# One decoder layer on one core: the last expert's order, its combines and the second LayerNorm rearranged, and larger weight transfers up to it

## The chip, the cores and the metric

The kernel runs on one core of a Trainium2 chip. The metric is device microseconds of one execution (us), less being better; the median of three runs before the change is 1119.88 us (1118.96 to 1120.91). The engines that matter here are TensorE (PE in the profile, its weight loads PEld), VectorE (DVE), ScalarE (ACT), GpSimd (POOL) and SyncE (SP), which issues nearly all DMAs.

## The reference, cut to what matters

For 256 tokens of width 1024, a mixing sublayer (two kinds of attention, merged and projected) is followed by a LayerNorm, and then by the sublayer in which the change lies:

```python
logits = (xt @ w_router + b_router)
top_val, top_idx = lax.top_k(logits, 4)              # 4 of 32 experts
gates = jax.nn.softmax(top_val, axis=-1)
# for each expert e and the tokens that chose it:
h = xb @ w_gate_up[e] + b_gate_up[e]                 # 1024 -> 2048
gate = jnp.minimum(gate, 7.0); up = jnp.clip(up, -7.0, 7.0)
act = gate * jax.nn.sigmoid(gate * 1.702) * (up + 1.0)
ys = act @ w_down[e] + b_down[e]                     # 1024 -> 1024
out[token] += ys * gate_weight
# and at the end
y = (xf - mu) * lax.rsqrt(var + LN_EPS) * g + b      # LN2 over alpha * h + moe(h)
```

Everything is float32. The weights of one expert are 8 MB of `w_gate_up` and 4 MB of `w_down`, so that 32 experts read 403 MB.

## The kernel before

**Experts.** A loop (`for e in range(NE)`) runs over 32 experts in order. Each one has room for 64 tokens; tokens beyond that go through a loop of their own after expert 20, which is skipped where there are none. An iteration issues on TensorE, in this order: `up_proj(e)` (eight steps c = 0 to 7, each a MB of weights and four logical products, which write two PSUM tiles G), `combine(e - 2)` (adds the output of the expert before the last to the four accumulators `acc[t][k]`, t for the half of the tokens, k for the half of the 1024 columns), `scatter` (two transposes that turn the weighted one-hot matrix into GT), half of a `gather` for the next pair of experts, the transposes of `swiglu(e)`, and `down(e - 1)`. A float32 product is two MATMUL records in the profile. A product with 64 output rows uses half of the array's columns, and two of them run side by side. After `up_proj`, ScalarE (L860) and VectorE (L858) copy the two tiles G to `G_sb`, which the transposes of `swiglu` read.

**Weights.** From expert 4's down weights on, weights lie in five buffers of 4 MB. An expert's `w_gate_up` is two tiles (the first with the steps c = 0 to 3, the second with 4 to 7), its `w_down` one. The list `items` holds them in the order of use: the two tiles of expert e, then the down tile of expert e - 1. `load_next` calls `fetch`, which issues a tile's DMAs on SP's queue, as soon as the tile five places earlier has been used. A tile goes as one DMA (32 KB in a row per partition), as two (16 KB) in the nine tiles from expert 28's first one to expert 29's down tile, and as four (8 KB) in the next three: the first and second up tile of expert 31, and the down tile of expert 30. A product waits for the DMA that brings the part it reads, not for the tile. The very last tile, the down weights of expert 31, is fetched in six pieces by `fetch_last`.

**The end.** After the loop, `down(31)` is written out in pieces: `last_down(k, c0, c1)` computes column half k for steps c0 to c1, into `pt[k]`, a PSUM tile of 128 x 256 whose upper 64 partitions hold the first 256 columns and whose lower ones the other 256. `last_combine(k)` copies it to both partition halves of D2 in four copies of 64 x 256, ScalarE and VectorE in turn, then TensorE adds D2 to the accumulators in two products of 64 rows and 512 columns, and VectorE takes the statistics of LN2 (`stats`: `bn_stats`, and with k = 1 the aggregate and ScalarE's square root). Then LN2 is applied to the four quarters (t, k) of the output. Three go through VectorE in two instructions each, `scaled` (L1074: subtract the mean, multiply by g) and `shifted` (L1078: multiply by the inverse deviation, add b), and the quarter (0, 1) through ScalarE (L1084) and two instructions of GpSimd (L1086). Each quarter is stored by a DMA of 256 KB.

**Order.** The schedule is manual: each engine runs its instructions in the order in which the program writes them, and waits only for the data they need. The framework that inserts the waits lets two engines use one PSUM bank only in turn.

Of the kernel before, what the change touches and what calls it, by code (L numbers as in the profile page):

```python
# [9 lines left out]
F32 = mybir.dt.float32  # L10
# [8 lines left out]
P = 128  # L19
# [16 lines left out]
def layer(tc, x, w_in, b_forget, sink, w_proj_swa, w_proj_fox, w_out, ln1_g, ln1_b, w_router, b_router,  # L36
# [9 lines left out]
    with ExitStack() as ctx:  # L46
# [71 lines left out]
        items += [("D", NE - 1, q) for q in range(2)]  # L118
        where, nxt, used, big = {}, [0], [0], []

        def fetch(kind, e, q, r, n=1, steps=1):

            src, m = (w_gate_up, 2) if kind == "G" else (w_down, 4)
            src = src[e].rearrange("a (p c) n -> p (a c) n", c=8)[:, m * q:m * q + m * n, :]
            dst, k = r.rearrange("p (c n) -> p c n", c=m * n), m * n // steps
            for i in range(0, m * n, k):
                sp.dma_start(dst[:, i:i + k], src[:, i:i + k])

        def fetch_last(r):

# [7 lines left out]
        def big_tile():  # L138

            return big[(nxt[0] - 2) // 2 % 5].tile([P, 2 * 4096], F32, name="ww", tag="ww")  # L140

        def load_next(n=1):
            for _ in range(n):
                i = nxt[0]
                kind, e, q = items[i]
                if i < SMALL:
                    r = extra.tile([P, 4096], F32, name="w") if i == 10 else slot_tile(slot_of[(i - (i > 10)) % 10])
                    where[kind, e, q] = r
                    fetch(kind, slice(e, e + 1), q, r)
                    nxt[0] += 1  # L150
                    continue
                r = big_tile()
                where[kind, e] = r
                for a in range(2):
                    where[kind, e, q + a] = r[:, 4096 * a:4096 * a + 4096]
                if i + 2 < len(items):
                    fetch(kind, slice(e, e + 1), q, r, 2, 4 if i + 8 >= len(items) else 2 if i + 26 >= len(items) else 1)
                else:
                    fetch_last(r)
                nxt[0] += 2  # L160
# [593 lines left out]
        with tc.tile_pool(name="mo", bufs=1) as mo:  # L754
# [85 lines left out]
                act.activation(GT, pt, AF.Copy)  # L840
                return GT

            def up_proj(xT_e, weights):
                G = [gp.tile([P, 512], F32, name="G") for _ in range(2)]
                for c in range(8):
                    if c % 2 == 0:
                        w = weights("G", c // 2).rearrange("p (c n) -> p c n", c=2)
                    for hf in range(2):
                        for k in range(2):
                            n0 = k * 1024 + hf * 512  # L850
                            pe.matmul(G[hf][64 * k:64 * k + 64, :], xT_e[:, c, :], w[:, c % 2, n0:n0 + 512],  # L851
                                      start=c == 0, stop=c == 7)
                G_sb = mo.tile([P, 8, P], F32, name="G_sb")
                for hf in range(2):
                    dst = G_sb.rearrange("q c p -> q p c")[:, 64 * hf:64 * hf + 64]
                    src = G[hf].rearrange("q (p c) -> q p c", c=8)
                    if hf:
                        dve.tensor_copy(dst, src)  # L858
                    else:
                        act.activation(dst, src, AF.Copy)  # L860
                return G_sb
# [34 lines left out]
            def combine(GT, D_sb, first=False):  # L896
                for t in range(2):
                    for k in range(2):
                        r = slice(64 * k, 64 * k + 64)
                        pe.matmul(acc[t][k], GT[r, t * P:(t + 1) * P], D_sb[r, :], start=first, stop=False)  # L900
# [65 lines left out]
            for e in range(NE):  # L966
                g = e // 2
                OHg = weighted(posm[:, :, e:e + 1], gate[:, :, e:e + 1])
                if e % 2 == 0 and e + 2 <= last:
                    OH = onehot(g + 1)  # L970
                G_sb = up_proj(xTs[g][:, :, e % 2, :], lambda kind, q: where[kind, e, q])
                refill(4, 2 if e == OVER else 0)

                if e > 1 and e != OVER + 1:
                    combine(GTs[e - 2], Ds[e - 2], e == 2)
                if e == NORM:
                    affine()
                    b_dn = mo.tile([NE, D], F32, name="rows")
# [6 lines left out]
                if e == REST:  # L985
# [13 lines left out]
                    rows = mo.tile([NE + 1, D], F32, name="rows")  # L999
                    act.dma_start(rows[0:1], ln2_g)  # L1000
                    act.dma_start(rows[NE:], ln2_b)
                GTs[e] = scatter(OHg)
                if 2 * (g + 1) <= last:
                    gather(g + 1, OH, 4 * (e % 2))
                aTs[e] = swiglu(G_sb, bT[:, :, :, e])
# [12 lines left out]
                if e == OVER:  # L1018
# [3 lines left out]
                    with tc.If(n_ov > 0):  # L1022
                        overflow()
                    refill(0)
            y = big_tile()[:, :2 * D].rearrange("p (t n) -> p t n", t=2)

            mv = mo.tile([P, 2, 2], F32, name="mv2")
            rs = mo.tile([P, 2], F32, name="rs2")
            nm = mo.tile([P, 1], F32, name="nm2")
            stt = mo.tile([P, 2, 2, 6], F32, name="stt2")  # L1030
            cs = [slice(512 * k, 512 * k + 512) for k in range(2)]

            def stats(t, k):
                dve.bn_stats(stt[:, t, k], acc[t][k])
                if k == 1:
                    dve.bn_aggr(mv[:, t], stt[:, t])
                    act.activation(rs[:, t:t + 1], mv[:, t, 1:2], AF.Sqrt, bias=eps)


            wv = where["D", last].rearrange("p (c n) -> p c n", c=8)  # L1040
# [9 lines left out]
            def last_combine(k):  # L1050

                D2 = mo.tile([P, 512], F32, name="tb", bufs=2)
                for r in (slice(0, 64), slice(64, P)):
                    act.activation(D2[r, :256], pt[k][:64], AF.Copy)  # L1054
                    dve.tensor_copy(D2[r, 256:], pt[k][64:])  # L1055
                for t in range(2):
                    r = slice(64 * t, 64 * t + 64)
                    pe.matmul(acc[t][k], GTs[last][r, t * P:(t + 1) * P], D2[r], start=False, stop=True)  # L1058
                for t in range(2):
                    stats(t, k)  # L1060

            for c in (0, 2, 4):
                for k in range(2):
# [2 lines left out]
                    combine(GTs[last - 1], Ds[last - 1])  # L1066
            last_down(0, 6, 8)
            last_down(1, 6, 7)
            last_combine(0)
            last_down(1, 7, 8)  # L1070
            last_combine(1)

            def scaled(t, k):
                dve.scalar_tensor_tensor(y[:, t, cs[k]], acc[t][k], mv[:, t, 0:1], gb[:, 0, cs[k]],  # L1074
                                         op0=OP.subtract, op1=OP.mult)

            def shifted(t, k):
                dve.scalar_tensor_tensor(y[:, t, cs[k]], y[:, t, cs[k]], rs[:, t:t + 1], gb[:, 1, cs[k]],  # L1078
                                         op0=OP.mult, op1=OP.add)
                sp.dma_start(out[t * P:(t + 1) * P, cs[k]], y[:, t, cs[k]])  # L1080

            dve.reciprocal(rs[:, 0:1], rs[:, 0:1])
            dve.scalar_tensor_tensor(nm, mv[:, 0, 0:1], -1.0, rs[:, 0:1], op0=OP.mult, op1=OP.mult)
            act.activation(y[:, 0, cs[1]], acc[0][1], AF.Identity, bias=nm, scale=rs[:, 0:1])  # L1084
            for a, op in ((0, OP.mult), (1, OP.add)):
                pool.tensor_tensor(y[:, 0, cs[1]], y[:, 0, cs[1]], gb[:, a, cs[1]], op=op)  # L1086
            scaled(0, 0)
            dve.reciprocal(rs[:, 1:2], rs[:, 1:2])
            shifted(0, 0)
            for k in range(2):  # L1090
                scaled(1, k)
                shifted(1, k)
            act.dma_start(out[0:P, cs[1]], y[:, 0, cs[1]])


_INS = ['x', 'w_in', 'b_forget', 'sink', 'w_proj_swa', 'w_proj_fox', 'w_out', 'ln1_g', 'ln1_b', 'w_router', 'b_router',
# [24 lines left out]
```

## Time and profile before

| | |
|---|---|
| median of the runs | 1119.88 us |
| profiled execution | 1119.41 us |
| its span, first to last instruction | 1117.2 us |
| PE busy | 1054.9 us (94%) |
| DVE / ACT / POOL busy | 378.3 / 211.3 / 4.8 us |
| TensorE's granted clock, mean | 0.985 of full speed |
| DMA, mean over the span | 387 GB/s; 429 to 432 in most slices of the expert loop |
| idle of PE ahead of `up_proj` (L851) | 19.5 us, of it 19.1 us for weights |

All times of the profile are counted from the first instruction; what the execution has beyond its span is 2.2 us. "Granted clock" is 1.00 at 2.4 GHz and 0.50 at 1.2 GHz. A busy PE means that a matmul is under way, not that the array is full. In a timeline a row is a run of like instructions, with the idle time before it and what ended that in brackets.

### The profile page before, as it was taken

What the parts mean: (1) busy time and instruction counts of PE and PEld (TensorE: products, weight loads), DVE (VectorE), ACT (ScalarE), POOL (GpSimd) and SP (SyncE); (2) the same over time, 40 slices, a digit from 0 to 9 for tenths busy, and PEclk for the clock granted to TensorE, in tenths of its full rate; (3) what the DMA queues carried; (4) which work ended last, traced back from release to release, by engine and by line L of the source; (5) the groups of instructions that cost most, each with busy time, mean ns of one, the idle gap of its engine ahead of it and who ended that gap; (6) DMA issues with size and microseconds to landing.
All of it is one profiled execution on the core that took longest, in us unless ns stands there. A gap on an engine that the chain in (4) does not pass through costs nothing. (4 is left out here: it accounts for less than half of the span.)

```text
span 1117.2 us, 13432 instructions
## 1 busy us (share of the span) xinstructions
PE 1054.9 (94%) x5677; PEld 517.1 (46%) x5677; DVE 378.3 (34%) x821; ACT 211.3 (19%) x416; POOL 4.8 (0%) x14
## 2 busy tenths in 40 slices
PE   9999999999999999999999999999998988998895
PEld 8988897533333333333333343333433333333322
DVE  5577476432222224222222222222222222222223
ACT  5466464311111110000000110011000000000011
POOL 0000000000000000000000000000000000000001
PEclk9999999999999998999999999999999999999997
DMA  9754599999999999999999999999999999999993
GB/s 274 227 195 146 140 392 354 377 426 405 429 424 429 432 431 416 430 429 430 430 430 431 429 432 431 431 431 430 429 429 431 430 429 430 426 425 428 423 419 121
DMA packets 46406, 432.48 MB, mean 387 GB/s; under 512 B 5524, under 2 KB 26020, under 8 KB 29448
## 3 DMA queue, kind: packets, MB, share of 16 engines
q1 hardware_dynamic: 46144, 431.18, 93.5%
q8 instruction: 46, 0.75, 0.3%
q10 hardware_dynamic: 200, 0.41, 0.1%
q14 instruction: 16, 0.13, 0.0%
HBM read 430.53 MB, written 1.05 MB: 386 GB/s over the span
## 5 line engine op out<-in xcount | busy, mean ns | idle before, releaser
L851 PE MATMUL G<-ww,xTe 128*64 128x512 f32 x1664 | 368.2, 597 | 19.5 <-DMA ww<-in_w_gate_up_dram 19.1
L851 PEld LDWEIGHTS G<-ww,xTe 128*64 128x64 f32 x1664 | 119.3, 138 | 264.1 <-issue 227.3
L886 PE MATMUL X<-ww,aT 128*64 128x512 f32 x864 | 191.3, 595 | 0.5 <-DVE tb L871 0.3
L858 DVE COPY G_sb<-G 128x512 f32<-128x512 f32 x32 | 33.2, 1037 | 408.0 <-PE G L851 408.0
L860 ACT ACTIVATE G_sb<-G 128x512 f32<-128x512 f32 x32 | 33.8, 1055 | 422.3 <-PE G L851 422.3
L886 PEld LDWEIGHTS X<-ww,aT 128*64 128x64 f32 x864 | 59.6, 137 | 113.4 <-issue 107.6
L851 PE MATMUL G<-w,xTe 128*64 128x512 f32 x384 | 83.5, 593 | 0.6 <-POOL nth L773 0.6
L312 PE MATMUL pj<-w 128*128 128x256 f32 x232 | 66.7, 288 | 1.3 <-ACT w L110 0.8
L314 PE MATMUL pj<-w 128*128 128x256 f32 x232 | 65.7, 283 | 0.2 <-DVE w L111 0.2
L313 PE MATMUL pj<-w 128*128 128x256 f32 x232 | 65.6, 283 | 0.0
L809 PE MATMUL X<-OH,h_perm 128*128 128x128 f32 x480 | 63.0, 288 | 1.2 <-DVE h_perm L947 0.9
L900 PE MATMUL acc<-D_sb,GT 64*128 64x512 f32 x248 | 61.6, 615 | 0.7 <-DVE D_sb L893 0.7
L809 PEld LDWEIGHTS X<-OH,h_perm 128*128 128x128 f32 x480 | 60.1, 204 | 1.8 <-PE X L839 1.2
L868 PE MATMUL X<-ident,G_sb 128*128 128x128 f32 x256 | 40.0, 280 | 20.1 <-ACT xTe L822 12.0
L873 ACT ACTIVATE sg<-tb 128x256 f32<-128x256 f32 x64 | 26.7, 416 | 148.5 <-DVE tb L872 148.5
L851 PEld LDWEIGHTS G<-w,xTe 128*64 128x64 f32 x384 | 28.3, 137 | 53.6 <-issue 52.3
L893 DVE COPY D_sb<-X 128x256 f32<-128x256 f32 x31 | 13.2, 425 | 112.0 <-ACT D_sb L892 112.0
L111 DVE TENSOR_TENSOR w<-w 128x1024 fp32r<-128x1024 f32 (+2 forms) x50 | 46.3, 965 | 13.8 <-ACT w L110 13.8
L312 PEld LDWEIGHTS pj<-w 128*128 128x128 f32 x232 | 44.3, 191 | 3.9 <-issue 2.2
L871 DVE TENSOR_TENSOR tb<-X,bT 128x512 f32<-128x512 f32 x64 | 43.7, 683 | 4.1 <-PE X L868 4.1
L314 PEld LDWEIGHTS pj<-w 128*128 128x128 f32 x232 | 44.4, 191 | 0.4 <-DVE w L111 0.4
L313 PEld LDWEIGHTS pj<-w 128*128 128x128 f32 x232 | 44.4, 191 | 0.0
(263 smaller groups left out, 866.6 us busy)
## 6 DMA issues: line engine op xcount, KB each, us to landing
ww<-in_w_gate_up_dram SPq DMA_DIRECT2D x44, 4096.0 KB, 27.2
ww<-in_w_down_dram SPq DMA_DIRECT2D x23, 4096.0 KB, 28.2
w<-in_w_gate_up_dram SPq DMA_DIRECT2D x24, 2048.0 KB, 10.0
ww<-in_w_gate_up_dram SPq DMA_DIRECT2D x12, 2048.0 KB, 38.5
w<-in_w_down_dram SPq DMA_DIRECT2D x8, 2048.0 KB, 10.7
w<-in_w_in_dram SPq DMA_DIRECT2D x14, 1024.0 KB, 5.6
ww<-in_w_down_dram SPq DMA_DIRECT2D x6, 2048.0 KB, 39.7
ww<-in_w_gate_up_dram SPq DMA_DIRECT2D x8, 1024.0 KB, 28.3
```

The source lines that it names most:

```text
L111: dve.tensor_tensor(lo, src, hi.bitcast(F32), op=OP.subtract)
L312: pe.matmul(pt[:, j, :], hi[:, c, cs], xh[:, c, :], start=c == 0, stop=False)
L313: pe.matmul(pt[:, j, :], hi[:, c, cs], xl[:, c, :], start=False, stop=False)
L314: pe.matmul(pt[:, j, :], lo[:, c, cs], xh[:, c, :], start=False, stop=c == 7)
L809: pe.matmul(pt[:, c, :], h_perm[:, t, c0 + c, :], OH[:, t].rearrange("p a s -> p (a s)"), start=t == 0, stop=t == 1)
L851: pe.matmul(G[hf][64 * k:64 * k + 64, :], xT_e[:, c, :], w[:, c % 2, n0:n0 + 512], start=c == 0, stop=c == 7)
L858: dve.tensor_copy(dst, src)
L860: act.activation(dst, src, AF.Copy)
L868: pe.transpose(pt[:, c].rearrange("p k s -> p (k s)"), G_sb[:, c0 + c, :], ident)
L871: dve.tensor_tensor(tb, pt, bias[:, c0:c0 + 4, :, None].to_broadcast([P, 4, 2, CAP]), op=OP.add)
L886: pe.matmul(pt[64 * k:64 * k + 64, :], aT[:, c, :], w[:, c % 4, k * 512:(k + 1) * 512], start=c == 0, stop=c == 7)
L900: pe.matmul(acc[t][k], GT[r, t * P:(t + 1) * P], D_sb[r, :], start=first, stop=False)
```

## The change

The diff has four parts. (1) Every weight tile up to expert 31's first up tile goes as one DMA; its second up tile goes as DMAs of 1, 1 and 2 MB; expert 30's down tile stays at four. (2) For the last expert alone, `combine(29)` and `scatter(31)` are issued inside `up_proj`, ahead of its step 6, rather than after it. (3) Both pieces of `last_down(1, ...)` come ahead of `last_combine(0)`, and each `last_combine` goes by column halves j: ScalarE and VectorE copy the same 64 x 256 piece of PSUM to D2's two partition halves, and then both tokens' halves t are added, 64 rows by 256 columns each. (4) In LN2, the quarters (0, 0), (0, 1) and (1, 0) are finished on TensorE: a PSUM tile `base` first gets the row b by a product with a row of ones (one row deep), a diagonal matrix of the inverse deviation times the scaled quarter is added to it, and ScalarE copies the sum out; the quarter (1, 1) stays on VectorE, and GpSimd has no part any more.

```diff
-        def fetch(kind, e, q, r, n=1, steps=1):
+        def fetch(kind, e, q, r, n=1, *parts):
...
-            dst, k = r.rearrange("p (c n) -> p c n", c=m * n), m * n // steps
-            for i in range(0, m * n, k):
-                sp.dma_start(dst[:, i:i + k], src[:, i:i + k])
+            dst, i, unit = r.rearrange("p (c n) -> p c n", c=m * n), 0, m * n // max(sum(parts), 1)
+            for k in parts or (1,):
+                sp.dma_start(dst[:, i:i + k * unit], src[:, i:i + k * unit])
+                i += k * unit
...
+                steps = {-6: (1, 1, 2), -4: (1, 1, 1, 1)}
...
-                    fetch(kind, slice(e, e + 1), q, r, 2, 4 if i + 8 >= len(items) else 2 if i + 26 >= len(items) else 1)
+                    fetch(kind, slice(e, e + 1), q, r, 2, *steps.get(i - len(items), (1,)))
...
-            def up_proj(xT_e, weights):
+            def up_proj(xT_e, weights, beside=None):
...
+                    if c == 6 and beside:
+                        beside()
...
+                def others():
+                    if e > 1 and e != OVER + 1:
+                        combine(GTs[e - 2], Ds[e - 2], e == 2)
+                    if e == last:
+                        GTs[e] = scatter(OHg)
+                G_sb = up_proj(..., others if e == last else None)
...
             def last_combine(k):
                 D2 = mo.tile([P, 512], F32, name="tb", bufs=2)
-                for r in (slice(0, 64), slice(64, P)):
-                    act.activation(D2[r, :256], pt[k][:64], AF.Copy)
-                    dve.tensor_copy(D2[r, 256:], pt[k][64:])
-                for t in range(2):
-                    r = slice(64 * t, 64 * t + 64)
-                    pe.matmul(acc[t][k], GTs[last][r, t * P:(t + 1) * P], D2[r], start=False, stop=True)
-                for t in range(2):
-                    stats(t, k)
+                for j in range(2):
+                    src, c = pt[k][64 * j:64 * j + 64], slice(256 * j, 256 * j + 256)
+                    act.activation(D2[:64, c], src, AF.Copy)
+                    dve.tensor_copy(D2[64:, c], src)
+                    for t in range(2):
+                        r = slice(64 * t, 64 * t + 64)
+                        pe.matmul(acc[t][k][:, c], GTs[last][r, t * P:(t + 1) * P], D2[r, c], start=False, stop=j > 0)
...
             last_down(1, 6, 7)
-            last_combine(0)
             last_down(1, 7, 8)
-            last_combine(1)
...
-            act.activation(y[:, 0, cs[1]], acc[0][1], AF.Identity, bias=nm, scale=rs[:, 0:1])
-            for a, op in ((0, OP.mult), (1, OP.add)):
-                pool.tensor_tensor(y[:, 0, cs[1]], y[:, 0, cs[1]], gb[:, a, cs[1]], op=op)
...
+            for k in range(2):
+                last_combine(k)
+                if k == 0:
+                    for t in range(2):
+                        stats(t, 0)
+            base = {}
+            for t, k in ((0, 0), (0, 1), (1, 0)):
+                base[t, k] = xp.tile([P, 512], F32, name="X") if t else gp.tile([P, 512], F32, name="G")
+                pe.matmul(base[t, k], ones[NE:NE + 1, :], rows[NE:NE + 1, cs[k]], start=True, stop=False)
+            diag = {}
+            def inverse(t):
+                dve.reciprocal(rs[:, t:t + 1], rs[:, t:t + 1])
+                diag[t] = mo.tile([P, P], F32, name="sg", bufs=2)
+                dve.tensor_scalar(diag[t], ident, rs[:, t:t + 1], None, op0=OP.mult)
+            def by_pe(t, k):
+                pe.matmul(base[t, k], diag[t], shifted[:, t, cs[k]], start=False, stop=True)
+                act.activation(y[:, t, cs[k]], base[t, k], AF.Copy)
+                store(t, k)
+            stats(0, 1)
+            scaled(0, 0)
+            inverse(0)
+            by_pe(0, 0)
+            stats(1, 1)
+            scaled(0, 1)
+            by_pe(0, 1)
+            inverse(1)
+            scaled(1, 0)
+            by_pe(1, 0)
+            scaled(1, 1)
+            dve.scalar_tensor_tensor(y[:, 1, cs[1]], shifted[:, 1, cs[1]], rs[:, 1:2], gb[:, 1, cs[1]],
+                                     op0=OP.mult, op1=OP.add)
+            store(1, 1)
```

## Rows read from the trace of the kernel before

**Rows 1.** Busy time by stretch; the last columns: granted clock, DMA share, GB/s
```profile
845.40:930.70 85.30, 76.96 (x384) 29.89 (x380) 21.68 (x47) 7.96 (x15) 0.00 (x0) 1.00 1.01 431
970.00:1050.00 80.00, 73.79 (x367) 28.41 (x367) 20.31 (x45) 6.56 (x14) 0.00 (x0) 1.00 1.01 427
1050.00:1078.00 28.00, 25.79 (x118) 8.19 (x114) 6.41 (x14) 2.65 (x5) 0.00 (x0) 1.00 1.01 418
```

**Rows 2.** Timeline of TensorE, experts 26 to 31: start, length, instruction, idle before
```profile
930.91 8.66 PE L851 MATMUL G<-ww,xTe 128*64 128x512 f32 x32 [3.04 <-DMA ww<-in_w_gate_up_dram]
...
951.94 7.04 PE L851 MATMUL G<-ww,xTe 128*64 128x512 f32 x32
...
1062.85 5.32 PE L851 MATMUL G<-ww,xTe 128*64 128x512 f32 x24
1068.56 1.94 PE L851 MATMUL G<-ww,xTe 128*64 128x512 f32 x8 [0.39 <-DMA ww<-in_w_gate_up_dram]
...
1078.52 1.94 PE L851 MATMUL G<-ww,xTe 128*64 128x512 f32 x8 [0.56 <-DMA ww<-in_w_gate_up_dram]
```

**Rows 3.** Timeline of all engines after the last up-projection
```profile
1080.39 1.99 PE L900 MATMUL acc<-D_sb,GT 64*128 64x512 f32 x8
1080.51 1.03 DVE L858 COPY G_sb<-G 128x512 f32<-128x512 f32 x1 [16.03 <-PE G L851]
...
1082.31 0.44 PE L839 MATMUL X<-ident,OHg 128*128 128x128 f32 x2
...
1083.96 7.09 PE L886 MATMUL X<-ww,aT 128*64 128x512 f32 x32
```

**Rows 4.** Timeline of all engines, last expert's combines to the end
```profile
1099.63 0.38 ACT L1054 ACTIVATE tb<-X 64x256 f32<-64x256 f32 x1 [8.09 <-PE X L1047]
1100.04 0.43 DVE L1055 COPY tb<-X 64x256 f32<-64x256 f32 x1 [8.04 <-ACT tb L1054]
...
1102.44 0.65 PE L1047 MATMUL X<-ww,aT 128*64 128x256 f32 x4
...
1104.10 2.94 PE L1058 MATMUL acc<-tb,GT 64*128 64x512 f32 x4 [1.00 <-DVE tb L1055]
...
1106.53 0.29 ACT L1037 ACTIVATE rs<-mv,eps 128x1 f32<-128x1 f32 x1 [2.08 <-DVE mv L1036]
...
1108.45 0.75 DVE L1074 SCALAR_TENSOR_TENSOR ww<-acc,mv,gb 128x512 f32<-128x512 f32 x1 [0.21 <-issue]
...
1111.07 3.45 SPq L1080 DMA_DIRECT2D out_dram<-ww  x3
```

**Rows 5.** VectorE by line from 800 us on: count, busy us, mean ns, idle before
```profile
L874 DVE TENSOR_SCALAR tb<-tb 128x256 f32<-128x256 f32 x22 | 6.5, 294 | 0.8
...
L1034 DVE BATCH_NORM_STATS2 stt<-acc 128x6 f32<-128x512 f32 x4 | 2.8, 698 | 1.7 <-PE acc L1058 1.7
```

**Rows 6.** One line's instructions, shortest, median and longest in ns
```profile
L1078 DVE SCALAR_TENSOR_TENSOR ww<-ww,rs,gb x3: 752/974/1807, 1109.2 to 1113.4; 128x512 f32<-128x512 f32 x3
```

**Rows 7.** Timeline of TensorE and ScalarE, experts 8, 14 and 16: nearest rows for new operations
```profile
425.15 1.98 PE L936 MATMUL X<-rows,ones 1*128 1x512 f32 x4
...
428.94 2.04 PE L936 MATMUL X<-rows,ones 1*128 1x512 f32 x2
...
591.71 7.07 PE L994 MATMUL acc<-h_perm,alpha_i 128*128 128x512 f32 x8
...
658.17 0.60 ACT L984 ACTIVATE gb<-X 128x512 f32<-128x512 f32 x1 [2.70 <-PE X L936]
```

**Rows 8.** Busy time by stretch (columns of rows 1), expert 16 and the tail
```profile
657.00:660.80 3.80, 3.80 (x11) 1.31 (x10) 0.00 (x0) 1.79 (x3) 0.00 (x0) 1.00 1.07 459
661.10:664.40 3.30, 2.98 (x14) 2.91 (x14) 0.00 (x0) 0.61 (x2) 0.00 (x0) 0.50 1.02 437
...
1101.40:1104.70 3.30, 2.30 (x9) 0.78 (x8) 2.04 (x4) 0.76 (x2) 0.00 (x0) 1.00 0.00 0
1104.80:1108.20 3.40, 2.24 (x3) 0.50 (x2) 2.08 (x7) 0.45 (x2) 0.00 (x0) 0.50 0.00 0
```

More of the change, by code (lines that the diff above doesn't have):

```diff
@@ L970, in layer @@
                     OH = onehot(g + 1)
-                G_sb = up_proj(xTs[g][:, :, e % 2, :], lambda kind, q: where[kind, e, q])
+                def others():
[3 more added lines that the diff above has]
+                        GTs[e] = scatter(OHg)
+                G_sb = up_proj(xTs[g][:, :, e % 2, :], lambda kind, q: where[kind, e, q], others if e == last else None)
                 refill(4, 2 if e == OVER else 0)
-                if e > 1 and e != OVER + 1:
-                    combine(GTs[e - 2], Ds[e - 2], e == 2)
+                if e < last:
+                    others()
                 if e == NORM:
@@ L1001, in layer @@
                     act.dma_start(rows[NE:], ln2_b)
-                GTs[e] = scatter(OHg)
+                if e < last:
+                    GTs[e] = scatter(OHg)
                 if 2 * (g + 1) <= last:
@@ L1024, in layer @@
                     refill(0)
-            y = big_tile()[:, :2 * D].rearrange("p (t n) -> p t n", t=2)
+            free = big_tile()
+            y, shifted = [free[:, 2 * D * i:2 * D * i + 2 * D].rearrange("p (t n) -> p t n", t=2) for i in range(2)]
             mv = mo.tile([P, 2, 2], F32, name="mv2")
             rs = mo.tile([P, 2], F32, name="rs2")
-            nm = mo.tile([P, 1], F32, name="nm2")
             stt = mo.tile([P, 2, 2, 6], F32, name="stt2")
             cs = [slice(512 * k, 512 * k + 512) for k in range(2)]
[L1033 to L1037, printed above, removed]
             wv = where["D", last].rearrange("p (c n) -> p c n", c=8)
@@ L1052, in last_combine, with stats, scaled, store @@
                 D2 = mo.tile([P, 512], F32, name="tb", bufs=2)
-                for r in (slice(0, 64), slice(64, P)):
-                    act.activation(D2[r, :256], pt[k][:64], AF.Copy)
-                    dve.tensor_copy(D2[r, 256:], pt[k][64:])
-                for t in range(2):
-                    r = slice(64 * t, 64 * t + 64)
-                    pe.matmul(acc[t][k], GTs[last][r, t * P:(t + 1) * P], D2[r], start=False, stop=True)
-                for t in range(2):
-                    stats(t, k)
+                for j in range(2):
[5 more added lines that the diff above has]
+                        pe.matmul(acc[t][k][:, c], GTs[last][r, t * P:(t + 1) * P], D2[r, c], start=False, stop=j > 0)
+            def stats(t, k):
+                dve.bn_stats(stt[:, t, k], acc[t][k])
+                if k == 1:
+                    dve.bn_aggr(mv[:, t], stt[:, t])
+                    act.activation(rs[:, t:t + 1], mv[:, t, 1:2], AF.Sqrt, bias=eps)
+            def scaled(t, k):
+                dve.scalar_tensor_tensor(shifted[:, t, cs[k]], acc[t][k], mv[:, t, 0:1], gb[:, 0, cs[k]],
+                                         op0=OP.subtract, op1=OP.mult)
+            def store(t, k):
+                sp.dma_start(out[t * P:(t + 1) * P, cs[k]], y[:, t, cs[k]])
             for c in (0, 2, 4):
@@ L1068, in layer @@
             last_down(1, 6, 7)
-            last_combine(0)
             last_down(1, 7, 8)
-            last_combine(1)
[L1073 to L1080, printed above, removed]
@@ L1082, in layer @@
-            dve.reciprocal(rs[:, 0:1], rs[:, 0:1])
-            dve.scalar_tensor_tensor(nm, mv[:, 0, 0:1], -1.0, rs[:, 0:1], op0=OP.mult, op1=OP.mult)
-            act.activation(y[:, 0, cs[1]], acc[0][1], AF.Identity, bias=nm, scale=rs[:, 0:1])
-            for a, op in ((0, OP.mult), (1, OP.add)):
-                pool.tensor_tensor(y[:, 0, cs[1]], y[:, 0, cs[1]], gb[:, a, cs[1]], op=op)
-            scaled(0, 0)
-            dve.reciprocal(rs[:, 1:2], rs[:, 1:2])
-            shifted(0, 0)
@@ L1090, in layer @@
[L1090 to L1093, printed above, removed]
+            for k in range(2):
[7 more added lines that the diff above has]
+                pe.matmul(base[t, k], ones[NE:NE + 1, :], rows[NE:NE + 1, cs[k]], start=True, stop=False)
```

## The prediction, made before the result was known

> **What bounds the kernel now.** The page's slices come first: in the expert loop the DMA engines are full and PE is nearly so, so two limits lie close together, and totals cannot tell which one a change meets. The windows give the stream's rate by packet size: 431 GB/s with 32 KB packets, 427 with 16 KB, 418 with 8 KB, at a DMA share of 1.01 in all three [rows 1]. The PE timeline tells who waits: up to expert 31's last up-projection step PE resumes when a transfer lands (1068.56, 1078.52) [rows 2]. After that no wait of PE for weights of any size appears: PE itself runs from the last landing to the end of `down(31)`, through the combine, scatter, transposes and `down(30)` [rows 3]. ScalarE's first copy at 1099.63 begins the last chain: copies, combines, statistics, LN2, and the last store's issue, which ends at 1111.07 + 3.45 = 1114.52, so starts near 1114.19 [rows 4]. Call 1099.63 minus its hop, 1099.55, T. T to the last store is 14.64 us. The sum is made against the profiled execution's 1119.41 us (span 1117.2 and 2.2 around it), 0.47 below the median of 1119.88.
>
> **Part 1, packets.** A tile of 4.19 MB takes 9.73 us at 431 GB/s, 9.82 at 427, 10.03 at 418 [rows 1]. Nine tiles gain 0.09, the first up tile of expert 31 gains 0.30: it lands whole 1.1 us earlier, at 1068.5 - 1.1 = 1067.4 (its last quarter released PE at 1068.56). The second up tile, half of it in a 2 MB piece, ends near 1077.3.
>
> The Trainium skill (DMA: Bandwidth & Descriptors, section Rules for kernel authors) asks for 128 partitions and at least 1 MiB per DMA for full bandwidth; all these sizes satisfy that, so by the rule this edit gains nothing and the forecast below would be 1.1 us higher, 1125.5. The rows differ by 3% between 1 MiB and 4 MiB pieces, and I go by them.
>
> But a product waits for the DMA that brings its part. Before, PE did expert 31's steps 0 to 2 from 1062.85 on while the quarters came in, and had eight MATMULs left to do at 1068.56 [rows 2]. Now steps 0 to 3 start at 1067.4 together. PE is not later than that for another reason: expert 30's second tile, also whole now, leaves 32 instead of 16 MATMULs behind its landing (+3.5 us, less 0.7 of earlier landing), so PE is free at 1062.85 + 2.8 = 1065.6. The like waits of about 2.7 us in experts 28 to 30 cost nothing, since each ends at a landing that comes anyway.
>
> **Part 2, combine and scatter ahead of step 6.** 32 MATMULs take 6.95 us (7.04 with the drain) [rows 2], combine and scatter 2.3 (1080.39 to 1082.7) [rows 3]. So: 1067.45 + 6.95 = 1074.4; steps 4 and 5, long landed, + 3.5 = 1077.9; combine and scatter 1080.2; steps 6 and 7, landed at 1077.3 and so not waited for, 1083.7. The move was to fill a wait, and there is none to fill. What it uncovers is the copy of G: VectorE's takes 1.03 us after the last product [rows 3] and was hidden behind the combine; now the transposes wait for it, to 1084.8. Before, they could start at the scatter's end, about 1082.75, and `down(30)` began 1.2 us later, at 1083.96; now it begins at 1084.8 + 1.3 = 1086.1. From there to T the PE work is the same, and all weights have landed. T moves by +2.2, to 1101.75. Bounds: if the clock falls in the 1.8 us of idle before 1067.4, +1.6 more (a stretch of 32 MATMULs after 3.04 us of idle took 8.66) [rows 2]; if no backlog arises and only the landing counts, 1077.3 + 3.5 + 1.1 gives 1081.9 for 1082.75, a gain, worked out as a rival.
>
> **Part 3, combines.** In the rows the four copies take turns: VectorE starts when ScalarE ends (1100.04 against 1099.63 + 0.38) and has no other reason to wait [rows 4]. The new pairs read the very same piece of one bank, so I take them as serial too: 4 x 0.45 = 1.8 us. (Side by side they would give back 0.9.) Products of half the columns for both t run side by side in 0.65, as the four MATMULs of 1102.44 do [rows 4]. Column half 0: T + 2.5; two `bn_stats` of 0.70 [rows 5] on VectorE, to T + 4.0, ahead of its copies for half 1; two VectorE copies with a ScalarE copy between, T + 5.3; product, T + 6.0 with the clock up, 6.5 with it down. Before it was 7.5 (1104.10 + 2.94 = 1107.04) [rows 4]. So this part gains 1.0 to 1.5.
>
> **Part 4, LN2.** It takes off VectorE three L1078, one of which needed 1807 ns beside GpSimd instead of 752 [rows 6], and one chain on GpSimd. It adds on PE, behind the last combine, three products one row deep and 512 wide. Two such took 1.98 us at full clock, one takes 2.04 at half [rows 7]: 2.9 to 6.1 us for three. Diagonal products have no row of their own; the same columns at one row deep give 0.99 and 2.04; the nearest rows of full depth, with a strided operand, 7.07 for four, 1.77 each [rows 7]. I take 0.99 and 2.04 by the clock.
>
> The order decides what this costs. ScalarE's square root for t = 1 is written behind the copy of quarter (0, 0), which needs the diagonal product, which stands behind all three base products; and VectorE stops at the reciprocal for t = 1 with (1, 0) and (1, 1) queued behind it. VectorE's own work up to there (0.70, 0.21, 0.75, 0.5) would be done 2.4 us after the last combine, so the base products are not hidden even at full clock.
>
> What is the clock? Before, it was 1.00 to 1104.7 and 0.50 from 1104.8 on, that is T + 5.2, after a stretch in which PE was busy 2.3 of 3.3 us; and in expert 16 PE was busy all of 657.0 to 660.8, with one-row products, and the clock was 0.50 in 661.1 to 664.4 [rows 8]. So idle and thin products bring it down, and the new tail has both: 2 us without a product from T + 2.5, then three one-row ones. The value I take: the first base product at full clock, the other two and the first two diagonal ones at half, the last diagonal one up again. (All of these at half is the upper bound, all at full the rival below.)
>
> Sum: last combine 1101.75 + 6.0 = 1107.75; base 0.99 + 2 x 2.04, 1112.8; diagonal (0, 0) 1114.85; its copy 0.65 (0.60 for 128 x 512 [rows 7] and a hop) 1115.5; square root 0.33 [rows 4] 1115.85; reciprocal and diagonal (0.29 is an upper bound [rows 5]) 0.5, 1116.35; `scaled(1, 0)` 0.78, 1117.1; product 0.99, 1118.1; copy, 1118.75; store issue 1118.8, and (1, 1)'s behind it on SP, 0.4 later, 1119.2. Before: 1114.19. That is +5.0, and 1119.41 + 5.0 = 1124.4 us. By part: head +2.2, combines -1.5, LN2 +4.3. All at half clock (combine T + 6.5): last store 1121.8, +7.6, 1127.0.
>
> **The rivals.** (1) *The clock stays up in the tail.* For it: the rows of the fall before had 64-row products one at a time, and the new ones stand in pairs. Place: base and diagonal products; it decides if the fall comes only after the last base product. Then: base done 1110.6, (0, 0) copied 1112.25, `scaled(1, 0)` 1113.85, last store 1115.95: +1.75, 1121.2 us, not slower by the bound below. Against it: the fall behind one-row products [rows 8]. The Trainium skill (TensorE: Matmul & The Clock Gate, section Loop structure matters more than you think) lets back-to-back matmuls keep the engine fast, which favours this rival, since the base products are back to back; expert 16's stretch speaks against reading it so.
> (2) *Landings, not PE, bound the last expert.* Then part 2 does what it seems to be for: the head ends at 1081.9 instead of 1082.75, T shifts by about -0.65 instead of +2.2, and the sum is 1124.4 - 2.85 = 1121.55. It needs expert 31's first tile 3 us ahead of 1067.4; the stream's 431 GB/s over 85 us [rows 1] leaves no room for that. For it: every one of PE's waits in that stretch ended at a landing [rows 2].
> Both together: 1121.2 - 2.85 = 1118.35.
> (3) *The copies do run side by side:* 0.9 less, 1123.5, in the forecast's range.
>
> **How the numbers follow.** A measurement of this kernel tells about 0.2% (2.2 us, so below 1117.6 or above 1122.1) from no change. Forecast with its clock mixes and rival 3: 0.60, 1122.3 to 1127.0, all slower. Rival 1: 0.16, same. Rival 2: 0.12, two thirds same, one third slower. Both: 0.07, half same, half faster. Unnamed: 0.05, faster. Faster 0.09, same 0.27, slower 0.64. The range takes in both rivals and all at half clock: 1119.0 to 1127.0.
>
> **What would show it.** Right: PE resumes expert 31's step 0 near 1067.4 after some 2 us of idle and doesn't wait in steps 4 to 7; the transposes of its `swiglu` wait for VectorE's copy; `down(30)` begins near 1086; the copies alternate; the granted clock is 0.50 during base products, each near 2 us; ScalarE's second square root starts behind the first 128 x 512 copy. Wrong: a wait at step 6 that combine and scatter fill; base products under 1 us each; a last store before 1116.

## The result and the profile after

The changed kernel takes 1125.56 us (median of five runs, 1125.11 to 1127.23) against 1119.88 before: ratio 1.0054, 95% interval 1.0040 to 1.0068, 4.5 to 7.6 us slower. The prediction was 1124.4 us, range 1119.0 to 1127.0. The profiled execution took 1126.7 us (span 1124.9); its rows are 1.1 us above the median.

TensorE around the last up-projection (columns of [rows 2]; answers to [rows 2, 3]):

```profile
1051.43 8.60 PE L856 MATMUL G<-ww,xTe 128*64 128x512 f32 x32 [2.63 <-DMA ww<-in_w_gate_up_dram]
...
1063.54 7.09 PE L891 MATMUL X<-ww,aT 128*64 128x512 f32 x32
1070.92 10.52 PE L856 MATMUL G<-ww,xTe 128*64 128x512 f32 x48 [0.29 <-DMA ww<-in_w_gate_up_dram]
1081.37 1.99 PE L905 MATMUL acc<-D_sb,GT 64*128 64x512 f32 x8
1083.29 0.44 PE L842 MATMUL X<-ident,OHg 128*128 128x128 f32 x2
1083.65 3.65 PE L856 MATMUL G<-ww,xTe 128*64 128x512 f32 x16
1088.52 1.07 PE L873 MATMUL X<-ident,G_sb 128*128 128x128 f32 x8 [1.21 <-DVE G_sb L863]
1089.94 7.09 PE L891 MATMUL X<-ww,aT 128*64 128x512 f32 x32 [0.35 <-DVE tb L876]
```

The 32 records of the first up tile all start behind 1070.92, when the tile is there; steps 4 to 7 wait for nothing, and the combine and scatter between 1081.37 and 1083.73 fill no gap. The transposes then wait 1.21 us for VectorE's copy of G, and `down(30)` 0.35 more. The chain of waits (start, length, piece) has that copy on the path that sets the end:

```profile
1029.39 41.48 DMA ww<-in_w_gate_up_dram
...
1083.72 3.61 PE G L856 x16
...
1087.36 1.03 DVE G_sb L863
...
1111.00 2.15 PE G L1098 x4
1113.15 1.71 PE X L1098 x2
1114.86 2.02 PE G L1107 x2
...
1116.90 0.60 ACT ww L1108
1117.49 0.19 ACT rs L1072
```

The tail in the timeline of all engines (answers to [rows 4]):

```profile
1105.60 0.38 ACT L1062 ACTIVATE tb<-X 64x256 f32<-64x256 f32 x1 [8.09 <-PE X L1054]
1106.01 0.42 DVE L1063 COPY tb<-X 64x256 f32<-64x256 f32 x1 [8.04 <-ACT tb L1062]
...
1107.63 1.30 DVE L1069 BATCH_NORM_STATS2 stt<-acc 128x6 f32<-128x512 f32 x2 [0.33 <-PE acc L1066]
...
1109.43 1.57 PE L1066 MATMUL acc<-tb,GT 64*128 64x256 f32 x6 [1.37 <-DVE tb L1063]
...
1110.93 2.22 PE L1098 MATMUL G<-rows,ones 1*128 1x512 f32 x4
...
1112.95 1.91 PE L1098 MATMUL X<-rows,ones 1*128 1x512 f32 x2
...
1114.79 3.78 PE L1107 MATMUL G<-ww,sg 128*128 128x512 f32 x4
...
1117.39 0.28 ACT L1072 ACTIVATE rs<-mv,eps 128x1 f32<-128x1 f32 x1
1117.52 4.19 SPq L1079 DMA_DIRECT2D out_dram<-ww  x4
1117.71 0.16 DVE L1102 RECIPROCAL rs<-rs 128x1 f32<-128x1 f32 x1 [3.39 <-ACT rs L1072]
```

The last combine ends at 1109.43 + 1.57 = 1111.00. The first two base products take 2.22 us together (four records), the third 1.91. VectorE idles 3.39 us until ScalarE's square root for t = 1, which stands behind the first quarter's copy.

Busy time by stretch (columns of [rows 1]; answers to [rows 8]): the clock is at 2.4 GHz through the combines, falls to 1.2 GHz while the second base product runs, stays there for 6.7 us, and is up again.

```profile
1106.00:1112.40 6.40, 5.03 (x24) 2.71 (x21) 4.58 (x10) 1.43 (x4) 0.00 (x0) 1.00 0.00 0
1112.60:1119.30 6.70, 6.36 (x8) 1.90 (x7) 3.24 (x8) 1.38 (x3) 0.00 (x0) 0.50 0.11 39
1119.50:1121.00 1.50, 0.74 (x2) 0.00 (x0) 0.76 (x2) 0.60 (x1) 0.00 (x0) 1.00 0.47 175
```

Four moments cut each execution into pieces: the start of expert 31's step 0, ScalarE's first copy in the last combines (T), the end of the last combine (U), the start of the last store's issue. The table has them for every kernel of this study (us, each from one profiled execution), and the ratio of all timed runs to those of the kernel before that were taken beside them (their medians are 1119.5 to 1120.0 us). What lies ahead of T is called the head.

| kernel | step 0 | step 0 to T | T to U | U to store | ratio (95%) |
|---|---|---|---|---|---|
| before | 1062.85 | 36.78 | 7.41 | 7.15 | |
| after | 1070.92 | 34.68 | 5.40 | 10.33 | 1.0054 (1.0040 to 1.0068) |
| e0_again | 1063.54 | 36.79 | 7.40 | 7.16 | 1.0007 (0.9999 to 1.0016) |
| e1_packets | 1067.45 | 33.13 | 6.45 | 7.15 | 1.0015 (1.0005 to 1.0025) |
| e2_beside | 1064.92 | 36.79 | 6.46 | 7.15 | 1.0006 (0.9997 to 1.0015) |
| e3_combines | 1063.56 | 36.79 | 5.39 | 6.66 | 0.9990 (0.9982 to 0.9999) |
| e4_ln2 | 1062.42 | 36.80 | 7.07 | 11.67 | 1.0044 (1.0031 to 1.0058) |
| e5_old_packets | 1063.64 | 36.79 | 5.40 | 10.33 | 1.0034 (1.0022 to 1.0046) |
| e6_after_up | 1066.77 | 33.12 | 5.92 | 11.68 | 1.0042 (1.0029 to 1.0056) |
| e7_tail_order | 1069.40 | 34.68 | 5.42 | 8.64 | 1.0037 (1.0025 to 1.0050) |
| e8_quarters | 1068.78 | 33.08 | 7.05 | 7.15 | 1.0006 (0.9996 to 1.0016) |
| e9_order | 1064.64 | 36.78 | 5.40 | 6.89 | 0.9985 (0.9975 to 0.9995) |
| e10_all | 1067.91 | 33.07 | 5.40 | 6.90 | 0.9983 (0.9971 to 0.9994) |
| e11_deep | 1067.40 | 34.68 | 5.40 | 9.55 | 1.0028 (1.0017 to 1.0039) |

Pieces behind step 0 repeat within 0.1 us between kernels that share their code and clock; step 0 itself does not: 1062.42 to 1064.92 in the seven kernels with the old packets.

### The profile page after: what moved, and what is told of

It reads as the page before. It is cut to its first block, busy times and chain, and to the rows that moved or that the text cites. A ratio compares the mean times of both kernels' runs of the same rounds, so it can differ in the third digit from the quotient of the medians.

```text
span 1124.9 us, 13454 instructions
## 1 busy us (share of the span) xinstructions
PE 1065.2 (95%) x5697; PEld 522.2 (46%) x5697; DVE 376.6 (33%) x821; ACT 212.3 (19%) x418; POOL 1.9 (0%) x12
```

## The experiments

**One part at a time, on the kernel before.** The theory is the prediction's: parts 1, 2 and 4 each cost, part 3 gains, each by its own step.

e0_again is the kernel before, unchanged, as a control.

> The kernel before, unchanged, once more. Theory A: how far the slowest DMA engine trails at the end (6.8 us in the trace of before, 9.1 in the changed kernel's) varies between executions of one program by some microseconds, and with it the time by up to 2 us. Theory B: it is 6.8 +- 0.3 again, and belongs to the program.

Its ratio of 1.0007 is what no change looks like here. By the completions in the traces, the slowest DMA engine trails the first by 7.8 us at the last weight transfer, against 6.8 in the trace of the kernel before. The difference of 1.0 us is beyond theory B's 0.3, so the trailing varies between executions of one program.

e1_packets has part 1 alone:

```diff
+                steps = {-6: (1, 1, 2), -4: (1, 1, 1, 1)}
...
-                    fetch(kind, slice(e, e + 1), q, r, 2, 4 if i + 8 >= len(items) else 2 if i + 26 >= len(items) else 1)
+                    fetch(kind, slice(e, e + 1), q, r, 2, *steps.get(i - len(items), (1,)))
```

> The kernel before with part 1 alone (the packets). Theory A (the prediction's): the stream gains about 1 us, but the products of steps 0 to 3 start together behind a whole tile and PE is left with a backlog; the head ends 2.0 us later after the landing and lands 1.1 earlier, so +0.9 to +1.1 us, about 1121.0; the slowest DMA engine trails the fastest as much as in executions of the kernel before. Theory B: 32 KB packets make the slowest engine trail more (the last up-projection tile landed 2.4 us later in the changed kernel than before, not 1.1 earlier): then +3 us or more, 1123 and above, and the trailing is seen in this run too.

TensorE's timeline of e1_packets:

```profile
1047.97 7.09 PE L854 MATMUL G<-ww,xTe 128*64 128x512 f32 x32 [2.48 <-DMA ww<-in_w_gate_up_dram]
...
1067.45 13.95 PE L854 MATMUL G<-ww,xTe 128*64 128x512 f32 x64 [1.80 <-DMA ww<-in_w_gate_up_dram]
```

TensorE idles 1.80 us, starts at 1067.45, and has 64 records in one stretch: the backlog of the prediction, at its time. Alone it costs 0.15%, as theory A had it; the slowest engine trails by 6.9 us, as in the kernel before (6.8), so theory B falls.

e2_beside has part 2 alone:

```diff
+                    if c == 6 and beside:
+                        beside()
...
+                G_sb = up_proj(xTs[g][:, :, e % 2, :], lambda kind, q: where[kind, e, q], others if e == last else None)
```

> The kernel before with part 2 alone (combine and scatter ahead of step 6 of the last up-projection). With quarters of a tile landing one by one PE still waits there, so the 2.3 us fill waits of 0.55 us each and uncover the copy of G: theory A gives -0.3 us, 1119.6, no change that can be told. Rival: the uncovered copy of 1.03 us costs in full, +0.8 to +1.1.

TensorE's timeline of e2_beside:

```profile
1075.61 1.94 PE L853 MATMUL G<-ww,xTe 128*64 128x512 f32 x8 [0.55 <-DMA ww<-in_w_gate_up_dram]
1077.48 1.99 PE L902 MATMUL acc<-D_sb,GT 64*128 64x512 f32 x8
1079.40 0.44 PE L839 MATMUL X<-ident,OHg 128*128 128x128 f32 x2
1079.77 3.65 PE L853 MATMUL G<-ww,xTe 128*64 128x512 f32 x16
1084.63 1.06 PE L870 MATMUL X<-ident,G_sb 128*128 128x128 f32 x8 [1.21 <-DVE G_sb L860]
1086.05 7.09 PE L888 MATMUL X<-ww,aT 128*64 128x512 f32 x32 [0.35 <-DVE tb L873]
```

With the old quarters there are waits to fill: the last 16 records need none, where before each 8 waited 0.5. What that saves, the uncovered copy (1.21) and the 0.35 behind it take back: step 0 to T is 36.79, as without the move. With the whole tile there is nothing to fill, and the move costs 34.68 - 33.13 = 1.55 us, the 1.21 + 0.35 of its two waits.

e3_combines has part 3 alone:

```diff
+                for j in range(2):
+                    src, c = pt[k][64 * j:64 * j + 64], slice(256 * j, 256 * j + 256)
+                    act.activation(D2[:64, c], src, AF.Copy)
+                    dve.tensor_copy(D2[64:, c], src)
```

> The kernel before with part 3 alone (combines by column halves). Theory A: last combine done 5.5 to 6.5 us after the first copy could start instead of 7.5: -1.0 to -2.0 us, about 1118.2. Rival: the two statistics that stand ahead of VectorE's copies for the second half take back what the shorter products give: 0.

The timeline of e3_combines:

```profile
1100.35 0.38 ACT L1055 ACTIVATE tb<-X 64x256 f32<-64x256 f32 x1 [8.09 <-PE X L1047]
1100.75 0.42 DVE L1056 COPY tb<-X 64x256 f32<-64x256 f32 x1 [8.04 <-ACT tb L1055]
...
1102.37 1.30 DVE L1034 BATCH_NORM_STATS2 stt<-acc 128x6 f32<-128x512 f32 x2 [0.33 <-PE acc L1059]
...
1104.17 1.57 PE L1059 MATMUL acc<-tb,GT 64*128 64x256 f32 x6 [1.37 <-DVE tb L1056]
```

The copies still take turns, and T to U falls to 5.39. It is the one part that gains: 0.1%, an effect as small as the control's 0.07% in the timed runs (interval 0.9982 to 0.9999), but plain in the pieces and found again in the two other kernels that have this part without part 4 (0.9985 and 0.9983).

e4_ln2 has part 4 alone, behind the old combines:

```diff
+            for t, k in ((0, 0), (0, 1), (1, 0)):
+                base[t, k] = xp.tile([P, 512], F32, name="X") if t else gp.tile([P, 512], F32, name="G")
+                pe.matmul(base[t, k], ones[NE:NE + 1, :], rows[NE:NE + 1, cs[k]], start=True, stop=False)
```

> The kernel before with part 4 alone (LN2 through TensorE, with the old combines). Theory A: the clock is at half from before the last combine on, base and diagonal products take about 2 us each, and the last store comes 9 to 13 us after the last combine instead of 7.15: +3.2 to +5.8 us, about 1124. Rival: the order alone costs and the clock does not matter, +1.5 to +2.

Here the clock is down before the first base product (a stretch of e4_ln2):

```profile
1105.00:1114.50 9.50, 9.50 (x12) 3.00 (x10) 3.28 (x8) 1.05 (x3) 0.00 (x0) 0.50 0.00 0
```

All three base products run at half clock, and U to the last store is 11.67 for 7.15: 4.5 us, most of the whole loss and more than the rival's 1.5 to 2.

**One part taken back.** e5_old_packets is the changed kernel with the old `fetch` and its old steps:

```diff
-                steps = {-6: (1, 1, 2), -4: (1, 1, 1, 1)}
...
+                    fetch(kind, slice(e, e + 1), q, r, 2, 4 if i + 8 >= len(items) else 2 if i + 26 >= len(items) else 1)
```

> The changed kernel with the packets of before (parts 2 to 4 alone). Theory A: the head goes back to what it was or 0.3 better, combines -2.0, LN2 +3.2: +0.9 against before, about 1120.8, so 4.7 us better than the changed kernel. Theory that the head's loss is mostly chance of the one trace: 1 to 2 us better than the changed kernel only, 1123.5 to 1124.5.

Step 0 to T is 36.79, as before, with part 2 still in: with the old packets the move costs nothing. The new packets cost 1.1 us by the mean starts (1068.39 + 33.13 against 1063.65 + 36.79, worked out below), and on top of them the move costs 1.55. The ratio is 0.2% or 2.2 us below the changed kernel's, between the two expectations, so the timed runs do not decide between them.

e6_after_up is the changed kernel without part 2:

```diff
-                G_sb = up_proj(xTs[g][:, :, e % 2, :], lambda kind, q: where[kind, e, q], others if e == last else None)
+                G_sb = up_proj(xTs[g][:, :, e % 2, :], lambda kind, q: where[kind, e, q], None)
...
-                if e < last:
-                    others()
+                others()
```

> The changed kernel with combine and scatter after the up-projection again (parts 1, 3 and 4). Theory A: the copy of G is covered again, 1.1 us better than the changed kernel, about 1124.5. Rival: there was a wait at step 6 that they filled, and it is 1 to 2 us worse.

Step 0 to T is 33.12, 1.56 shorter than in the changed kernel, as theory A had it. In this execution the clock fell during the last combine already (T to U 5.92), and LN2 took 11.68 for 10.33: the same code, 1.35 us by the clock alone. A stretch of e6_after_up (columns of [rows 1]) and its first two base products, to set against the changed kernel's 2.22:

```profile
1105.00:1114.50 9.50, 9.50 (x12) 3.09 (x11) 3.83 (x11) 1.07 (x3) 0.00 (x0) 0.50 0.00 0
```

```profile
1105.74 3.78 PE L1097 MATMUL G<-rows,ones 1*128 1x512 f32 x4
```

e7_tail_order is the changed kernel with two base products ahead of the second combine, and ScalarE's square root for t = 1 ahead of its first 128 x 512 copy:

```diff
+                        based(0, t)
+            based(1, 0)
...
             inverse(0)
+            stats(1, 1)
             by_pe(0, 0)
-            stats(1, 1)
```

> The changed kernel with two of the three base products between the two combines, and the square root for t = 1 ahead of the first copy on ScalarE. Theory A: the diagonal product (0, 0) no longer waits for base products and VectorE no longer waits for that copy: 1.5 to 2.5 us better than the changed kernel, about 1123.5. Rival: the half clock alone sets the tail and the order does not matter: 0 to 0.5.

The timeline of e7_tail_order:

```profile
1106.46 1.98 PE L1093 MATMUL G<-rows,ones 1*128 1x512 f32 x4
...
1112.70 0.29 ACT L1072 ACTIVATE rs<-mv,eps 128x1 f32<-128x1 f32 x1 [1.89 <-DVE mv L1071]
```

Two base products go where TensorE waited for copies anyway, T to U stays 5.42, and U to the last store drops from 10.33 to 8.64. So the order made 1.7 of LN2's 3.2 us in these executions, and not the clock, which fell 0.3 us after U here and 1.5 after it in the changed kernel; 8.64 is still 1.5 more than the old LN2.

**What was left open.** Is it the whole tile that costs in part 1, with a real gain in the stream? e8_quarters is the kernel before with part 1, but both up tiles of expert 31 in quarters:

```diff
+                steps = {-8: (1, 1, 1, 1), -6: (1, 1, 1, 1), -4: (1, 1, 1, 1)}
```

> The kernel before with part 1, but both up tiles of expert 31 (and expert 30's down tile) go as four DMAs of 1 MB, so that only the nine tiles before them change. Theory A: what part 1 cost was the whole first up tile, which kept TensorE idle until 1067.4 and left 32 matmuls in a backlog, while the nine tiles' stream gain (9 x 0.09 us) is real: the copy of the last expert starts about 0.8 us earlier than before, ratio about 0.999, 1118.7 us beside 1119.5 for before. Rival: the packet size gains nothing at this place; ratio 1.000. Rival 2: the loss was in the packets themselves; like e1_packets, ratio 1.0015.

1120.95 us beside 1120.0: theory A's 0.999 is outside the interval, and the rival that the packets gain nothing in time stands. So does rival 2: e1_packets' 1.0015 is inside the interval, and the timed runs cannot show that the quarters gave anything back. TensorE's timeline of e8_quarters shows what became of them in this execution:

```profile
1049.63 8.73 PE L854 MATMUL G<-ww,xTe 128*64 128x512 f32 x32 [2.63 <-DMA ww<-in_w_gate_up_dram]
...
1068.78 13.90 PE L854 MATMUL G<-ww,xTe 128*64 128x512 f32 x64
```

The backlog has moved one tile up. Expert 30's second tile lands whole at 1049.63 and leaves 32 records, which take 8.73 us for 7.09 as the clock fell; from there to T TensorE never waits for weights, so the whole backlog is on the path to T, and the 1.6 us that the clock took with it.

Does LN2 on VectorE lose time to GpSimd, and can the order save it? e9_order is the kernel before with part 3, and both `scaled(1, k)` ahead of the three `shifted`:

```diff
+            for k in range(2):
+                scaled(1, k)
             shifted(0, 0)
             for k in range(2):
-                scaled(1, k)
                 shifted(1, k)
```

> The kernel before with part 3, and in its old LN2 both scaled(1, k) come ahead of the three shifted on VectorE. Theory A: a shifted beside GpSimd's work is what takes up to 1.8 us, so moving the PSUM-reading scaled there and the shifted behind GpSimd's work saves about 0.7 us on top of part 3's 1.1: last combine to last store about 6.0 instead of 6.66, ratio about 0.9985, 1117.7 us. Rival: the slow stretch just meets the other instruction; last combine to last store stays at 6.7, ratio 0.999 as e3_combines.

One line of e9_order, shortest, median and longest in ns (the view of [rows 6]):

```profile
L1079 DVE SCALAR_TENSOR_TENSOR ww<-ww,rs,gb x3: 740/742/1749, 1110.6 to 1112.9; 128x512 f32<-128x512 f32 x3
```

The slow one is still there, 1749 ns for 742: U to the last store is 6.89 against e3_combines' 6.66, so the order saved nothing, as the rival had it. The ratio of 0.9985 is that of e3_combines (0.9990) within the intervals, so part 3 alone can account for it. The two instructions `scaled` that ran beside GpSimd's took 1.39 us together. The Trainium skill (SBUF — State Buffer, section Who interferes with whom) says that a VectorE instruction contends with a GpSimd instruction that reads SBUF when it has two SBUF inputs, and not when it has at most one and is outside its two-port modes; the rows agree, since `scaled` reads one of its two tensors from PSUM and `shifted` both from SBUF.

e10_all is e8_quarters and e9_order in one kernel, both edits as above.

> e8_quarters and e9_order in one kernel. Theory A, terms add: -0.8 (packets) -1.1 (combines) -0.7 (order of LN2) = -2.6 us against the kernel before, about 1116.9 us, ratio 0.9977, faster than both kernels. Rival: only the combines gain, ratio 0.999, 1118.4 us.

1118.3 us beside 1120.0: ratio 0.9983 (0.9971 to 0.9994), below the kernel before, by some 1.9 us of the expected 2.6. It cannot be told from e3_combines or e9_order; part 3, which all three have, accounts for the gain.

Does depth set the clock? e11_deep is the changed kernel with base products 128 rows deep:

```diff
-                pe.matmul(base[t, k], ones[NE:NE + 1, :], rows[NE:NE + 1, cs[k]], start=True, stop=False)
+                pe.matmul(base[t, k], ident, gb[:, 1, cs[k]], start=True, stop=False)
```

> The changed kernel, with its three base products 128 rows deep (identity times the broadcast row b) instead of one row deep; everything else is as it was. Theory A: thin products bring the clock down in the tail, so it stays at 1.00 through the base and the diagonal products, whose span shrinks; last combine to last store 8.7 instead of 10.3, about 1.6 us better than the changed kernel, 1124.0 us, ratio to before 1.004. Rival: what the array does in the idle time and the combines ahead has already decided the clock, and depth does not matter: it falls to 0.50 about 1.5 us after the last combine, 10.3, 1125.6 us, ratio 1.0054.

Stretches of e11_deep; its last combine ends at 1107.48:

```profile
1106.00:1107.30 1.30, 1.30 (x6) 0.79 (x6) 0.67 (x2) 0.27 (x1) 0.00 (x0) 1.00 0.00 0
1107.50:1110.70 3.20, 3.20 (x4) 1.42 (x5) 2.90 (x8) 0.29 (x1) 0.00 (x0) 0.50 0.00 0
1110.90:1116.00 5.10, 3.86 (x9) 1.25 (x7) 2.31 (x5) 1.39 (x4) 0.00 (x0) 1.00 0.28 103
```

Neither side was right. The clock falls all the same, as the first base product starts at 1107.41, where the changed kernel's fell 1.5 us after U; but it is back after 3.4 us instead of 6.8, so that U to the last store is 9.55 for 10.33. The base products' depth cannot have caused a fall that comes with their start; what stood ahead was the combines with their waits. Nor does the fall need base products at all: by the clock records in the traces it comes between 2.8 us before U and 1.7 us after it in all fourteen kernels of the table, and eight of them have none. That depth brings the clock back sooner fits this execution and the five with thin products (down for 6.8 us in the changed kernel, e5_old_packets and e7_tail_order, for 10.2 in e4_ln2 and e6_after_up), but rests on one execution of deep products and is not settled. The timed gain, 1.0028 for 1.0054, is larger than the 0.8 us of the tail; where the rest lies was not found.

## Why the prediction was right, and where its terms were off

Slower by its own steps, within the range. From step 0 to the last store every step was found; against the profiled execution the terms came out as follows (predicted, measured):

- **Head: +2.2, +5.97** (T 1099.63 to 1105.60). The mechanism (whole tile, backlog, no wait to fill, copy uncovered) is all there. One small step was left out: `down(30)` starts 19.02 us after step 0 where the prediction had 1086.1 - 1067.45 = 18.65, since TensorE also waits 0.35 for VectorE's `tb`. The larger miss, 3.5 us, is step 0 itself: 1070.92 for 1067.4. e1_packets and e11_deep have 1067.45 and 1067.40, so the forecast is what one execution can give, but the whole-tile kernels go up to 1070.92 (mean of e1, e6, e7, e11 and the changed kernel 1068.39). With the mean old start of 1063.65 the head is 1068.39 + 34.68 - 1063.65 - 36.79 = +2.63.

  The stream did gain its 1.1 us. By the completions in the traces, averaged over the 16 DMA engines, expert 31's first up tile is complete 137.65 us after expert 26's second, up to which the packets are the same, in each of the seven kernels with the old packets, and 136.55 after it in each of the five with the new ones (136.80 in e8_quarters and e10_all). But a product waits for the slowest engine. In the changed kernel against the one before, the average was 1.37 us later at expert 26 already, the packets took 1.10 off, and the slowest engine trailed the average by 5.10 instead of 3.00: the tile landed 2.37 later, not 1.1 earlier. The prediction took the trailing of one trace for every execution. Expert 30's second tile was late too (1051.43 for e1_packets' 1047.97) and its records ran partly at half clock, so that TensorE was busy until 1070.63 and idled 0.29 where the prediction had some 2 us (1.80 in e1_packets). The rates by stretch, 431, 427 and 418 GB/s [rows 1], became 430, 431 and 421:

```profile
845.40:930.70 85.30, 80.33 (x384) 31.13 (x386) 21.68 (x47) 7.96 (x15) 0.00 (x0) 0.96 1.00 430
970.00:1050.00 80.00, 72.75 (x364) 28.50 (x360) 21.34 (x46) 7.97 (x15) 0.00 (x0) 1.00 1.00 431
1050.00:1078.00 28.00, 26.15 (x116) 9.00 (x118) 6.40 (x14) 2.65 (x5) 0.00 (x0) 0.94 0.99 421
```

- **Combines: -1.5, -2.0.** T + 5.4 for T + 6.0. The copies are serial, as taken (rival 3 falls). The term off is the statistics: the pair starts when the first of the two products is done, at T + 2.03, and takes 1.30, where the prediction had it start after both and take 1.40 [rows 5].
- **LN2: +4.3, +3.2.** The clock falls 1.5 us after the last combine, not 1.0, so two base products ran nearly at full clock and only the third at half: the base was done at U + 3.86, not U + 5.05, and the sign "each near 2 us" held for one of three. Where exactly it falls is chance: in e6_after_up, the same code from T on, it fell 1.3 us ahead of U. Of the reason given for the fall, idle and thin products, the thin ones are not needed, since it comes without them too (at 1104.8, ahead of U, in the kernel before [rows 8]). ScalarE's late square root, VectorE's stop and the quarter (1, 0) on the path came as told. With the clock down earlier, e6_after_up has 11.68 where the prediction had 11.45.

The sum: 5.97 - 2.01 + 3.18 = 7.14 for +5.0. By the mean starts it is 2.6 - 2.0 + 3.2 = 3.8, a little below what the timed runs gave (4.5 to 7.6); what made the changed kernel's five runs that much later was not found, though an earlier fall of the clock, as in e6_after_up, would be 1.35 of it. So it is partly luck that 1124.4 lies this near to 1125.56: the head came out higher than forecast, combines and LN2 lower. In the timed runs the four parts account for the whole as far as these can tell: their ratios, each known to about 0.1%, multiply to 1.0055 against 1.0054. With one part of it taken back the ratio is 1.0034 (packets), 1.0042 (move) and 1.0037 (order of the tail).

Rival 1 falls by the 6.7 us at 0.50, though two of the three base products came ahead of them. The Trainium skill (TensorE: Matmul & The Clock Gate, section Loop structure matters more than you think) lets back-to-back matmuls keep the engine fast; here the clock fell at 1112.5 though TensorE had worked without a gap since 1109.43, so being back to back did not keep it up. Nor did it bring it up at once: TensorE was busy 6.36 of the 6.70 us at half clock, and 3.20 of 3.20 in e11_deep. Rival 2 falls by 1081.37 to 1083.65: nothing to fill.

## What to carry to other kernels

Where consumer and stream are nearly equally fast, choose the size of the last tiles by what a whole tile leaves behind its landing, and not by the stream's rate alone: here the rate gave 1.1 us in all, and the backlog of 16 more MATMUL records took more than that back. Work moved into a gap pays only if the gap is still there after the other edits, and the instruction it used to cover must be looked up first (1.55 us here). In a tail like this one, where the clock fell in every trace, work taken to TensorE is best priced at half clock. And where the arrival of data moves by several us, an edit is best measured between events of one trace, which here repeat to 0.1 us as long as the clock does the same.

## What was not expected of the hardware

The arrival of one tile depends on the slowest of the 16 DMA engines: TensorE starts at 1070.92, and the last of the tile's 16 completions is at 1070.88. By the completions in the traces, the engines finish expert 31's first up tile between 1061.73 and 1070.88 in the changed kernel and between 1060.96 and 1067.36 in e11_deep, the same transfers: 9.15 and 6.40 us apart, with the first ones 0.8 apart. The two ends of the stream show it, after first, then e11_deep (columns of [rows 1]): the last bytes come 2 us later, at a DMA share of 0.13, two engines of 16.

```profile
1096.00:1098.00 2.00, 1.89 (x14) 0.72 (x10) 0.42 (x1) 0.38 (x1) 0.00 (x0) 1.00 0.43 163
1098.00:1100.00 2.00, 1.98 (x12) 0.98 (x14) 0.00 (x0) 0.00 (x0) 0.00 (x0) 1.00 0.13 39
```

```profile
1096.00:1098.00 2.00, 2.00 (x14) 0.81 (x12) 0.00 (x0) 0.00 (x0) 0.00 (x0) 1.00 0.14 50
1098.00:1100.00 2.00, 2.00 (x22) 1.35 (x20) 0.00 (x0) 0.00 (x0) 0.00 (x0) 1.00 0.00 0
```

At the last weight transfer the spread is 6.4 to 9.1 us over the traces, with old packets (8.4 in e2_beside) and new (6.9 in e1_packets) alike. It is not made there: it grows over the whole stream, from 3.2 us at 324 us and 6.0 at 621 to 9.1 in the changed kernel, and from 1.5 and 3.4 to 6.4 in e11_deep. What sets it was not found. Against e11_deep it is 2.75 of the 3.5 us by which the tile came later.

A wait of about 2.6 us ahead of a whole tile sometimes brings the clock down: 32 records took 8.60 us in the changed kernel after 2.63 us of idle, 8.73 in e8_quarters after the same, but 7.09 in e1_packets after 2.48 and in e6_after_up after 2.64.
